# The opening of a two-layer conditioned decoder trunk: statistics first, all transposes ahead of the products, modulation pieces in pairs of quarters, a first chunk of six tiles

## The chip, the cores and the metric

The program runs on one core of one Trainium2 chip. The time is the device time of one execution in microseconds (us); lower is better. Engines are named as in the profile: PE is the matrix engine, DVE the vector engine, ACT the scalar engine, POOL the third elementwise engine, SP the engine whose queue issues most transfers (DMA).

## The reference

The reference is one inference step of a trunk of two layers, width 1024, over 256 prompt rows and 64 sample rows (8 samples of 8 rows), 320 rows in all. Each layer is a gated feed-forward block, four mixers side by side, and a second feed-forward block, each after a modulation whose scale, shift and gate come from a conditioning vector c, and each followed by a layer norm. The change touches only what happens before and in the first products of the first feed-forward block. Cut to that:

```python
def layer_norm(x, g, b, eps=1e-5):
    mu = jnp.mean(x, axis=-1, keepdims=True)
    var = jnp.mean(jnp.square(x - mu), axis=-1, keepdims=True)
    return (x - mu) * lax.rsqrt(var + eps) * g + b
def modulate(x, shift, scale):
    return x * (1.0 + scale[:, None, :]) + shift[:, None, :]
def swiglu(x, w_gate, w_up, w_down):
    return (jax.nn.silu(x @ w_gate) * (x @ w_up)) @ w_down
...
x = layer_norm(x, ln_in_g, ln_in_b)
for l in range(DEPTH):
    ada = (silu(c) @ w_ada[l] + b_ada[l]).reshape(b_, N_ADA, D_MODEL)
    sh1, sc1, g1, sh2, sc2, g2, sh3, sc3, g3 = [ada[:, i] for i in range(N_ADA)]
    h = swiglu(modulate(x, sh1, sc1), ffn1_w_gate[l], ffn1_w_up[l], ffn1_w_down[l])
    x = layer_norm(ALPHA * x + 0.5 * (1.0 + g1)[:, None, :] * h, post_ln_g[l, 0], post_ln_b[l, 0])
    ...
```

## The kernel before

All matrices are cut into tiles of 128 by 128. The 320 rows of x lie along the free axis and the 1024 features on the partitions, as eight tiles (k = 0 to 7) of 128x320. Each product is done in three matmuls, because weights and inputs are split into a high and a low part: high times high, low weight times high input, and high weight times low input. The tile names are `whi`, `wlo` for the weights and `xhi`, `xlo` for the inputs (`xhif`, `xlof` in the first feed-forward block).

The weights come from memory in the order in which the products use them. One load of 1 MB (`raw<-in_w_main`, called a pair here) holds two units of eight tiles each; a unit is split by one cast on ACT (`whi`, line 226) and one subtraction on DVE (`wlo`, line 234). The conditioning weights come as loads of 1 MB as well (`raw<-in_w_ada`, called pieces). SP issues all of them in one fixed order (`START = "aawaawaawaa"`, a for a piece, w for a pair), each when one of five buffers is free (`Stream.pump`).

The order of the instructions on every engine is the order in which the Python code calls them, and each engine works its queue off in that order. `next_unit`, which `tile` calls when a unit is used up, also splits units ahead by the table `AHEAD = (2, 2, 4, 4, 7, 8, 10)`: when unit 4 begins, units up to number 6 must be split, and those that aren't yet are split there.

The opening runs as follows. `setup` loads x with rows on the partitions (`xt`, three tiles), adds 1 to the bias table of the conditioning (`par`, two instructions on DVE, which wait for its load), then takes statistics of x and normalises it. `turn(k)` transposes feature tile k on PE (three matmuls into `xtp`), and `land(k)` copies it into SBUF. For the first feed-forward block the scale and the shift are made in quarters of 256 features: each quarter takes two pieces. One piece is 32 matmuls in the profile (`adp`, line 454, two calls of `ada_mm`), a copy by ACT (`adev`), and matmuls with a selection matrix (`adp<-sel,adev`, line 482, one selection for both pieces), whose result DVE adds to the bias table (line 491). From it `quarter(q)` makes A and B on DVE, then the modulated input tiles 2q and 2q+1: for the first of them ACT makes `xhi` directly, then come both `xff`, the second `xhi`, and DVE makes the two `xlo`.

`zchunk0` runs the first chunk: `kouter` goes over the eight k, and for each k over five weight tiles, each with its own PSUM bank (`zcf`, six banks in the ring `mm`). For one k it issues ten matmuls with `xhi`, then five with `xlo`. Between them lie the pieces of the next quarter, the selection and the last two transposes. After the odd k, `split_until(FIRST[q])` splits units up to 4, 6 and 7. After the chunk, `proj` makes the sixth tile (`uf`, m = 2) by itself, and the tiles from m = 3 on.

## Time and profile before

| | |
|---|---|
| three runs | 1305.42, 1308.83, 1309.57 us; median 1308.83 |
| span of the profiled execution, first to last instruction | 1308.1 us |
| PE busy | 1280.0 us, 98% of the span |
| DVE busy | 724.4 us, 55% |
| ACT busy | 556.6 us, 43% |
| mean granted clock of PE | 0.981 of full |

The page gives the span of the profiled execution, and no time of its own around it; the median of the runs lies 0.7 us above that span. A busy PE is a PE with a matmul in flight, whatever its clock.

### The profile page before, as it was taken

The page shows a single profiled execution, that of the slowest core. Times are in us where ns is not written, and L with a number is a line of the kernel's source. Part 1 is how long each engine was busy: PE and PEld are TensorE (multiplying, and loading weights), DVE is VectorE, ACT ScalarE, POOL GpSimd, SP SyncE. Part 2 cuts the span into 40 slices and gives each one's busy share as a digit, 9 for nine tenths or more (in the row PEclk, how much of TensorE's full clock was granted, in tenths as well). Part 3 has the DMA queues.
Part 4 walks back from the last instruction along what each step waited for, and adds up shares of the span by engine and source line. Part 5 has one row for each costly group of instructions (what it writes and reads, how often), then busy time and mean ns, then how long its engine had stood idle before and what let it go on. Part 6 is the DMA issues. An engine that isn't in the chain of part 4 may idle for free.

```text
span 1308.1 us, 22265 instructions
## 1 busy us (share of the span) xinstructions
PE 1280.0 (98%) x9382; PEld 1217.7 (93%) x9382; DVE 724.4 (55%) x1315; ACT 556.6 (43%) x878; POOL 33.4 (3%) x53
## 2 busy tenths in 40 slices
PE   6999999999999999999999999999999999999997
PEld 4999999989888999999999999999887999999997
DVE  4644444457976644444465444444697775444443
ACT  3643333337344633333445434333553455443432
POOL 0000000010010000000000000000100000000000
PEclk9999999999999999999999999999898989999998
DMA  9765656557879554554455454545387794444401
GB/s 353 275 233 206 211 193 237 207 159 247 325 259 121 188 202 178 199 185 163 166 185 196 164 183 172 190 174 180 113 287 286 115 197 157 140 158 152 143 29 41
DMA packets 51492, 247.46 MB, mean 189 GB/s; under 512 B 18656, under 2 KB 21168, under 8 KB 22208
## 3 DMA queue, kind: packets, MB, share of 16 engines
q1 hardware_dynamic: 46432, 244.33, 56.2%
q8 instruction: 73, 1.20, 0.4%
q0 software_dynamic: 512, 0.86, 0.4%
q10 hardware_dynamic: 4448, 0.84, 0.3%
q14 instruction: 27, 0.22, 0.1%
HBM read 243.45 MB, written 2.57 MB: 188 GB/s over the span
## 4 chain that ended last, share of the span: by engine, by line
PE 96%; DVE 1%; DMA 1%; ACT 1%; issue 0%; POOL 0%; SPq 0%; POOLq 0%; ACTq 0%; DVEq 0%
PE adp L459 4%; PE of L676 4%; PE oh L676 4%; PE oh L677 4%; PE of L677 4%; PE of L678 4%; PE oh L678 4%; PE uf L676 4%; PE uh L676 4%; PE uh L678 4%; PE uf L678 4%; PE uh L677 4%; PE uf L677 4%; PE gf L676 4%; PE gh L676 3%; PE gf L677 3%
## 5 line engine op out<-in xcount | busy, mean ns | idle before, releaser
L234 DVE TENSOR_TENSOR wlo<-raw,whi 128x1024 fp32r<-128x1024 f32 x312 | 372.8, 1222 | 135.9 <-ACT whi L226 134.6
L226 ACT CAST whi<-raw 128x1024 fp32r<-128x1024 f32 x312 | 315.6, 1045 | 28.7 <-issue 9.2
L676 PE MATMUL of<-hhf,whi 128*128 128x320 f32 x352 | 109.6, 311 | 0.0
L676 PE MATMUL oh<-hhh,whi 128*128 128x320 f32 x352 | 109.0, 310 | 0.0
L678 PE MATMUL of<-hhf,wlo 128*128 128x320 f32 x352 | 108.8, 309 | 0.0
L677 PE MATMUL of<-hlf,whi 128*128 128x320 f32 x352 | 108.8, 309 | 0.0
L678 PE MATMUL oh<-hhh,wlo 128*128 128x320 f32 x352 | 108.7, 309 | 0.0
L677 PE MATMUL oh<-hlh,whi 128*128 128x320 f32 x352 | 108.7, 309 | 0.0
L676 PE MATMUL uf<-xhif,whi 128*128 128x320 f32 x320 | 99.6, 311 | 0.0
L676 PE MATMUL uh<-xhih,whi 128*128 128x320 f32 x320 | 99.0, 309 | 0.0
L677 PE MATMUL uf<-xlof,whi 128*128 128x320 f32 x320 | 98.8, 309 | 0.0
L678 PE MATMUL uh<-xhih,wlo 128*128 128x320 f32 x320 | 98.8, 309 | 0.0
L677 PE MATMUL uh<-xloh,whi 128*128 128x320 f32 x320 | 98.8, 309 | 0.0
L678 PE MATMUL uf<-xhif,wlo 128*128 128x320 f32 x320 | 98.8, 309 | 0.0
L676 PE MATMUL gf<-xhif,whi 128*128 128x320 f32 x304 | 94.7, 312 | 0.0
L676 PE MATMUL gh<-xhih,whi 128*128 128x320 f32 x304 | 94.4, 310 | 0.0
L677 PE MATMUL gh<-xloh,whi 128*128 128x320 f32 x304 | 93.8, 309 | 0.0
L677 PE MATMUL gf<-xlof,whi 128*128 128x320 f32 x304 | 93.8, 309 | 0.0
L678 PE MATMUL gf<-xhif,wlo 128*128 128x320 f32 x304 | 93.8, 309 | 0.0
L678 PE MATMUL gh<-xhih,wlo 128*128 128x320 f32 x304 | 93.8, 309 | 0.0
L779 ACT CAST hhf<-sgf 128x320 fp32r<-128x320 f32 x44 | 20.2, 459 | 135.0 <-DVE sgf L776 135.0
L779 ACT CAST hhh<-sgh 128x320 fp32r<-128x320 f32 x44 | 20.2, 460 | 134.0 <-DVE sgh L776 134.0
(349 smaller groups left out, 2835.0 us busy)
## 6 DMA issues: line engine op xcount, KB each, us to landing
raw<-in_w_main SPq DMA_DIRECT2D x156, 1024.0 KB, 5.0
raw<-in_w_ada SPq DMA_DIRECT2D x72, 1024.0 KB, 4.9
out_yT<-x SPq DMA_DIRECT2D x8, 160.0 KB, 1.8
xt<-in_x SPq DMA_DIRECT2D x2, 512.0 KB
wsT<-in_wsT SPq DMA_DIRECT2D x2, 256.0 KB, 6.0
sgln<-in_sgln SPq DMA_DIRECT2D x2, 256.0 KB
cD<-in_pre_d POOLq DMA_DIRECT2D x4, 120.0 KB, 6.1
out_o_ds<-cD ACTq DMA_DIRECT2D x4, 120.0 KB
```

The source lines that it names most:

```text
L226: kk.nc.scalar.copy(hi, raw)
L234: self.kk.nc.vector.tensor_tensor(lo, raw, hi, op=ALU.subtract)
L459: nc.tensor.matmul(ps[32 * g:32 * g + 32, 0:w], self.cs[:, k, :], wt[:, h, g * w:(g + 1) * w], start=(k == 0), stop=(k == NK - 1))
L676: mm(ps, hi, xh, start=first, stop=False)
L677: mm(ps, hi, xl, start=False, stop=False)
L678: mm(ps, lo, xh, start=False, stop=last)
L779: nc.scalar.copy(hi, sg)
```

## The change

It changes the opening in five places.

- The two additions to the bias table come after the statistics and the normalisation of x in DVE's queue.
- All eight tiles of x are transposed ahead of the first product: two after the first piece, two after the second, four after the selection. Tiles 6 and 7 had their turn inside the first chunk before. `land` now says which engine copies.
- Ahead of the products stand two pieces where there were three.
- The two pieces of the next quarter are run one after the other, after the even k, and the selection and `quarter` lie inside the odd k, after the first three of its weight tiles; before, one piece lay ahead of the even k, one in it, and the selection ahead of the odd k.
- The first chunk has six tiles per k instead of five, so that each unit holds other tiles, and `uf` for m = 2 is made in it.

```diff
+CH0 = 6
...
-        for l in range(L):
-            a0 = PC[f"b_ada{l}"][0]
-            v = self.par[:, a0:a0 + 72].rearrange("p (i s k) -> p i s k", s=3, k=8)[:, :, 1:3, :]
-            nc.vector.tensor_scalar(v, v, 1.0, None, op0=ALU.add)
...
             nc.vector.tensor_scalar(xt[b][:n], xt[b][:n], mv[:n, b, 0:1], rs[:n, 3 + b:4 + b],
                                     op0=ALU.subtract, op1=ALU.mult)
+        for l in range(L):
+            a0 = PC[f"b_ada{l}"][0]
+            v = self.par[:, a0:a0 + 72].rearrange("p (i s k) -> p i s k", s=3, k=8)[:, :, 1:3, :]
+            nc.vector.tensor_scalar(v, v, 1.0, None, op0=ALU.add)
...
         st.ada(2)
         self.ada_adv(1)
+        turn(0)
+        land(0)
+        turn(1)
+        land(1)
         st.ada(2)
-        turn(0)
-        turn(1)
+        self.ada_adv(1)
+        turn(2)
+        turn(3)
+        land(2, True)
+        land(3)
         todo = st.split_hi(1)
         self.ada_adv(2)
-        land(0)
-        land(1)
         self.ada_adv(3)
-        for k in range(2, 6):
+        for k in range(4, 8):
             turn(k)
...
-    def kouter(self, x, banks, first, last, mid=None):
+    def kouter(self, x, banks, first, last, mid=None, at=None):
...
-        for w, b in zip(ws, banks):
+        for i, (w, b) in enumerate(zip(ws, banks)):
+            if mid and i == at:
+                mid()
             mm(b, w[0], xh, start=first, stop=False)
             mm(b, w[1], xh, start=False, stop=False)
-        if mid:
-            mid()
...
-        for k in range(2, 6):
-            land(k)
+        for k in range(4, 8):
+            land(k, k % 2 == 0)
         st.split_until(2)
-        banks = [self.mm(f"zc{nm}{i}") for i in range(CH)]
-        def piece():
-            st.ada(2)
-            self.ada_adv(1)
+        banks = [self.mm(f"zc{nm}{i}") for i in range(CH0)]
 
         for q in range(4):
-            if q < 3:
-                piece()
-            self.kouter(self.xk(2 * q), banks, q == 0, False, piece if q < 3 else None)
-            if q < 3:
+            def params():
                 self.ada_adv(3)
                 quarter(q + 1)
-            self.kouter(self.xk(2 * q + 1), banks, False, q == 3)
-            if q < 2:
-                turn(6 + q)
-                land(6 + q)
+
+            self.kouter(self.xk(2 * q), banks, q == 0, False)
+            if q < 3:
+                st.ada(4)
+                self.ada_adv(1)
+            self.kouter(self.xk(2 * q + 1), banks, False, q == 3, params if q < 3 else None, CH0 // 2)
             if q < 3:
                 st.split_until(FIRST[q])
...
-            if m == 2:
-                pg = b[4]
-            else:
-                pg = self.proj(self.mm(f"g{nm}{m}"))
-            glu(m, pg, self.proj(self.mm(f"u{nm}{m}")))
+            pg = b[2 * m] if 2 * m < len(b) else self.proj(self.mm(f"g{nm}{m}"))
+            pu = b[2 * m + 1] if 2 * m + 1 < len(b) else self.proj(self.mm(f"u{nm}{m}"))
+            glu(m, pg, pu)
...
-        tiles += _ffn_tiles(a["ffn1_w_gate"][l], a["ffn1_w_up"][l], a["ffn1_w_down"][l], CH)
+        tiles += _ffn_tiles(a["ffn1_w_gate"][l], a["ffn1_w_up"][l], a["ffn1_w_down"][l], CH if l else CH0)
```

**First place: PE, from its first instruction.** `adp` is a piece, `xtp` a transposed tile, `xt_72` to `xt_74` the three tiles of x. Before:

```order
L454 MATMUL adp_127<-raw_86,cs 32x128 x16
L454 MATMUL adp_148<-raw_88,cs 32x128 x16
L376 MATMUL xtp_167<-ident,xt_72 128x128
L376 MATMUL xtp_167<-ident,xt_73 128x128
L376 MATMUL xtp_167<-ident,xt_74 128x64
L376 MATMUL xtp_171<-ident,xt_72 128x128
L376 MATMUL xtp_171<-ident,xt_73 128x128
L376 MATMUL xtp_171<-ident,xt_74 128x64
L482 MATMUL adp_127<-sel,adev_146 128x18
L482 MATMUL adp_148<-sel,adev_179 128x18
```

Now:

```order
L459 MATMUL adp_127<-raw_86,cs 32x128 x16
L377 MATMUL xtp_148<-ident,xt_72 128x128
L377 MATMUL xtp_148<-ident,xt_73 128x128
L377 MATMUL xtp_148<-ident,xt_74 128x64
L377 MATMUL xtp_154<-ident,xt_72 128x128
L377 MATMUL xtp_154<-ident,xt_73 128x128
L377 MATMUL xtp_154<-ident,xt_74 128x64
L459 MATMUL adp_160<-raw_88,cs 32x128 x16
L377 MATMUL xtp_181<-ident,xt_72 128x128
L377 MATMUL xtp_181<-ident,xt_73 128x128
```

The two first transposes moved ahead of the second piece.

**Second place: PE, where the first chunk uses the second pair of weights for the first time** (`whi_353` before, `whi_366` now; `adp<-sel` is the selection from which the next tiles' parameters come). Before, this is in k = 3, after the selection of the third quarter:

```order
L690 MATMUL zcf_249<-xlof_328,whi_239 128x320
L482 MATMUL adp_363<-sel,adev_382 128x18
L482 MATMUL adp_394<-sel,adev_413 128x18
L685 MATMUL zcf_245<-xhif_318,whi_239 128x320
L686 MATMUL zcf_245<-xhif_318,wlo_240 128x320
L685 MATMUL zcf_246<-xhif_318,whi_353 128x320
L686 MATMUL zcf_246<-xhif_318,wlo_354 128x320
L685 MATMUL zcf_247<-xhif_318,whi_353 128x320
```

Now it is the fifth weight tile of k = 2, in the second quarter:

```order
L693 MATMUL zcf_258<-xhif_338,wlo_252 128x320
L692 MATMUL zcf_259<-xhif_338,whi_251 128x320
L693 MATMUL zcf_259<-xhif_338,wlo_252 128x320
L692 MATMUL zcf_260<-xhif_338,whi_251 128x320
L693 MATMUL zcf_260<-xhif_338,wlo_252 128x320
L692 MATMUL zcf_261<-xhif_338,whi_366 128x320
L693 MATMUL zcf_261<-xhif_338,wlo_367 128x320
```

The selection of the second quarter stands 20 products ahead of that row now. ACT's queue from that selection on reads the same as before, with other numbers: the two copies of pieces, `quarter`, and behind them the casts of the second pair:

```order
L483 COPY adev_319<-adp_281 128x128
L483 COPY adev_321<-adp_300 128x128
L651 ACTIVATE xhif_338<-x_189,B_220,A_219 128x256
L654 CAST xhif_338<-xff_337 128x64
L651 ACTIVATE xff_337<-x_189,B_220,A_219 128x256
L651 ACTIVATE xff_339<-x_191,B_220,A_219 128x256
L657 CAST xhif_340<-xff_339 128x320
L227 CAST whi_366<-raw_144 128x1024
L227 CAST whi_370<-raw_144 128x1024
```

The use of the second pair moved nearer to the selection, its casts did not.

**Third place: DVE, at the parameters of the fourth quarter** (line 491, now 496; `raw_267` before and `raw_298` now is the third pair of weights, `raw_411` the fourth). Before:

```order
L234 TENSOR_TENSOR wlo_467<-raw_267,whi_466 128x1024
L234 TENSOR_TENSOR wlo_471<-raw_267,whi_470 128x1024
L491 TENSOR_TENSOR ada_105<-adp_476,par 128x18
L491 TENSOR_TENSOR ada_105<-adp_507,par 128x18
L514 TENSOR_TENSOR A_207<-ada_105,par 128x18
L515 TENSOR_TENSOR s_537<-ada_105,par 128x18
```

Now:

```order
L235 TENSOR_TENSOR wlo_480<-raw_298,whi_479 128x1024
L235 TENSOR_TENSOR wlo_484<-raw_298,whi_483 128x1024
L235 TENSOR_TENSOR wlo_550<-raw_411,whi_549 128x1024
L496 TENSOR_TENSOR ada_103<-adp_507,par 128x18
L496 TENSOR_TENSOR ada_103<-adp_526,par 128x18
L519 TENSOR_TENSOR A_219<-ada_103,par 128x18
```

The low part of unit 6, first of the fourth pair, moved ahead of the two additions; on ACT its cast moved ahead of the fourth quarter in the same way. It is `next_unit` that puts it there: unit 4 now begins with the third weight tile of k = 5, just ahead of that selection.

## Rows read from the trace of the kernel before

**Rows 1.** Page, part 4: the chain that ended last, shares by engine.

```profile
PE 96%; DVE 1%; DMA 1%; ACT 1%; issue 0%; POOL 0%; SPq 0%; POOLq 0%; ACTq 0%; DVEq 0%
```

**Rows 2.** Timeline, PE, opening: start us, length, line, tiles, count, [idle before, releaser].

```profile
11.40 1.94 PE L454 MATMUL adp<-raw,cs 128*32 128x128 f32 x32 [11.40 <-DMA raw<-in_w_ada]
13.80 1.93 PE L454 MATMUL adp<-raw,cs 128*32 128x128 f32 x32 [0.46 <-DMA raw<-in_w_ada]
15.66 1.90 PE L376 MATMUL xtp<-ident,xt 128*128 128x128 f32 x6
...
18.36 3.70 PE L376 MATMUL xtp<-ident,xt 128*128 128x128 f32 x12
22.00 1.93 PE L454 MATMUL adp<-raw,cs 128*32 128x128 f32 x32
23.86 0.64 PE L685 MATMUL zcf<-xhif,whi 128*128 128x320 f32 x1
```

**Rows 3.** Timeline, PE, first chunk: the same columns.

```profile
24.56 0.47 PE L685 MATMUL zcf<-xhif,whi 128*128 128x320 f32 x1
...
26.43 0.47 PE L686 MATMUL zcf<-xhif,wlo 128*128 128x320 f32 x1
26.82 1.08 PE L454 MATMUL adp<-raw,cs 128*32 128x128 f32 x32
27.84 1.00 PE L690 MATMUL zcf<-xlof,whi 128*128 128x320 f32 x5
28.68 0.52 PE L482 MATMUL adp<-sel,adev 128*128 128x18 f32 x4
...
29.27 0.30 PE L686 MATMUL zcf<-xhif,wlo 128*128 128x320 f32 x1
...
30.44 0.31 PE L686 MATMUL zcf<-xhif,wlo 128*128 128x320 f32 x1
...
32.84 0.41 PE L685 MATMUL zcf<-xhif,whi 128*128 128x320 f32 x1
33.09 0.31 PE L686 MATMUL zcf<-xhif,wlo 128*128 128x320 f32 x1
...
51.07 0.37 PE L406 MATMUL bmean<-apar,o 128*128 128x112 f32 x2
51.21 0.39 PE L676 MATMUL uf<-xhif,whi 128*128 128x320 f32 x1
...
54.82 0.31 PE L676 MATMUL gf<-xhif,whi 128*128 128x320 f32 x1
```

**Rows 4.** Timeline, DVE, input statistics: the same columns.

```profile
8.07 0.28 DVE L346 TENSOR_SCALAR par<-par 128x48 f32<-128x48 f32 x2 [6.85 <-DMA par<-in_par]
...
11.12 1.23 DVE L357 BATCH_NORM_STATS2 bsx<-xt 64x6 f32<-64x512 f32 x2
...
13.78 2.25 DVE L363 TENSOR_SCALAR xt<-xt,mvx,rsx 128x1024 f32<-128x1024 f32 x3 [1.00 <-POOL rsx L360]
```

**Rows 5.** Timeline, ACT, second quarter of the modulation: the same columns.

```profile
27.97 0.27 ACT L478 COPY adev<-adp 128x128 f32<-128x128 f32 x1 [3.71 <-PE adp L454]
...
30.46 0.23 ACT L649 CAST xhif<-xff 128x64 fp32r<-128x64 f32 x1
...
32.08 2.00 ACT L226 CAST whi<-raw 128x1024 fp32r<-128x1024 f32 x2
```

**Rows 6.** Timeline, DVE, second quarter of the modulation: the same columns.

```profile
29.00 0.40 DVE L491 TENSOR_TENSOR ada<-adp,par 128x18 f32<-128x18 f32 x2 [4.27 <-PE adp L482]
...
33.16 2.36 DVE L234 TENSOR_TENSOR wlo<-raw,whi 128x1024 fp32r<-128x1024 f32 x2
```

**Rows 7.** Page, part 6: loads of the weights, KB each, us to landing.

```profile
raw<-in_w_main SPq DMA_DIRECT2D x156, 1024.0 KB, 5.0
```

**Rows 8.** Timeline, PE, after the first mixer: the columns of rows 2.

```profile
422.34 0.42 PE L685 MATMUL zch<-xhih,whi 128*128 128x320 f32 x1 [2.01 <-ACT xhih L649]
```

**Rows 9.** Windows: us, busy (count) by engine, PEclk, DMA share, GB/s.

```profile
419.00:422.50 3.50, 1.49 (x19) 0.71 (x19) 2.59 (x8) 0.97 (x3) 0.00 (x0) 0.95 0.88 335
422.50:426.00 3.50, 3.50 (x15) 3.50 (x16) 2.98 (x12) 3.33 (x7) 0.00 (x0) 0.54 0.99 405
```

More of the change, by code (lines that the diff above doesn't have):

```diff
@@ L367, in setup @@
         st.keep = 999
-        zs = []
+        zs = [None] * NK
         pts = {}
@@ L376, in turn, with land @@
                 nc.tensor.transpose(pt[:, b * P:b * P + n], xt[b][:n, k * P:(k + 1) * P], self.ident[:n, :n])
-        def land(k):
-            z = c.tile([P, N], F32, tag="res", bufs=8, name=f"x{k}")
-            if k % 2:
+        def land(k, act=False):
+            z = zs[k] = c.tile([P, N], F32, tag="res", bufs=8, name=f"x{k}")
+            if act:
                 nc.scalar.copy(z, pts.pop(k)[:, 0:N])
@@ L383, in land @@
                 nc.vector.tensor_copy(z, pts.pop(k)[:, 0:N])
-            zs.append(z)
         st.ada(2)
         self.ada_adv(1)
+        turn(0)
+        land(0)
+        turn(1)
+        land(1)
         st.ada(2)
-        turn(0)
-        turn(1)
+        self.ada_adv(1)
[3 more added lines that the diff above has]
+        land(3)
         todo = st.split_hi(1)
         self.ada_adv(2)
-        land(0)
-        land(1)
         self.ada_adv(3)
-        for k in range(2, 6):
+        for k in range(4, 8):
             turn(k)
-        return zs, todo, turn, land
+        return zs, todo, land
     def setup2(self):
@@ L719, in zchunk, with zchunk0 @@
         return banks
-    def zchunk0(self, nm, gb, todo, turn, land):
+    def zchunk0(self, nm, gb, todo, land):
         st = self.st
```

## The prediction

> **What bounds the kernel now.** I read three views in this order. First the chain of work that ended last: PE carries 96% of it [rows 1], so only time that PE waits, works at a low clock, or spends on switching counts. Then PE's timeline of the opening [rows 2]. PE starts at 11.40 us with the first piece, pauses 0.46 us for the load of the second, and from 13.80 on has no idle time in the opening: two transposes, selection, four transposes, third piece, first product at 23.86. What the change can save there is that pause and the order of the work behind it. Last the spacing of the products [rows 3], which tells the clock. From 24.56 to 26.43 seven products of 128x320 are 0.267 us apart, which is 320 columns at 1.2 GHz; from 29.27 to 30.44 eight are 0.147 apart, the level of 2.4 GHz. Pieces show the same: 1.86 us at 22.00, 1.02 at 26.82. So the clock rose at about 26.8, some 2.9 us after the first product.
>
> I compare one point before and after: the first product of `gf` for m = 3, at 54.82 before [rows 3]. Ahead of it lie the same 144 products either way (120 in the chunk and 24 of `uf` before, 144 in the chunk now), 8 pieces, 8 transposed tiles, 4 selections.
>
> **To the first product.** Taken out: the pause (0.46) and the third piece, 22.00 to 23.86 (1.86). Added: two transposed tiles, at 3.64 us for four (18.36 to 22.00), 1.82 [rows 2]. The first product comes at 23.86 - 0.46 - 1.86 + 1.82 = 23.36.
>
> This needs x normalised when the first piece ends, at 13.26. Before, the third tile's statistics began at 11.12, in an unbroken run behind the two additions of 8.07, and the three normalised tiles were done from 13.78 to 16.03 [rows 4]. The loads of x stand ahead of the pieces in SP's queue, and two pieces land 2.4 us apart (11.40, 13.80); by that estimate x is there at 9.0. The statistics then end 2.1 us earlier and the third tile is normalised at 13.9, when PE, at 0.30 us a transpose, asks for it (13.26 + 0.61). I take no wait. If nothing moved, PE would wait to 15.66, 2.4 us; those are the bounds. The two additions themselves (0.28 us) now stand ahead of DVE's first copies, while PE transposes; without that cover they cost 0.28.
>
> **The first quarter.** With the clock up at 26.8 as before, 12.9 products go by at 0.267, the other 5.1 of the 18 take 0.75: 27.55. Two pieces at 1.02 [rows 3] end at 29.59. Six products behind a piece take 0.25 for the first (32.84 to 33.09) and 0.147 for the others: 0.98. The selection, called s, starts at 30.57.
>
> From one selection to the next, without a wait: the start of the second product comes 0.59 after s (28.68 to 29.27), the twelfth ends at s + 2.21, 18 products of the even k take 2.65, two pieces 2.04, six products 0.98: 7.88. Two such steps, then 2.21, 36 products (5.29) and the bias means (51.07 to 51.21, 0.14) end at 30.57 + 15.76 + 2.21 + 5.29 + 0.14 = 53.97. Against 54.82 that is a **gain of 0.85 us**, from the pause and from fewer switches between pieces and products.
>
> **First wait: the second pair of weights.** The new order uses it in the fifth weight tile of k = 2, at s + 2.21 + 8 x 0.147 = s + 3.38, its low part at s + 3.53. ACT casts it behind the whole second quarter and DVE subtracts behind both `xlo`. Those queues are as before, so I read them from s = 28.68: the modulated tile is cast at 30.69 (s + 2.01) and ACT begins the pair at 32.08 [rows 5]; DVE begins its subtractions at 33.16 and ends the first of the two, half of 2.36 us, at 34.34 [rows 6], which is s + 5.66. PE, there at s + 3.53, waits **2.13 us**, in two parts around one product. Before, this pair was first used after the next two pieces, and the same work was hidden. The tile k = 2 itself is in time: s + 2.01 against s + 2.21. Units 4 and 5 are first wanted 7.6 us after the selection behind which they are cast (2.21 + 2.65 + 2.04 + 0.25 + 3 x 0.147), so there is no wait. Bounds: none if PE came 2.13 us later, 2.3 with a hand-over.
>
> **Second wait: unit 6 ahead of the fourth quarter.** ACT's copy of the last piece starts 0.13 us after the piece's end and takes 0.27 (27.84, 27.97), so it ends at s - 0.58; the cast of unit 6 (half of 2.00 us) ends at s + 0.42, DVE's subtraction starts 0.08 later (33.16 against 33.08) and takes 1.18: s + 1.68. The additions for the quarter, due at s + 0.32 (29.00 against 28.68), are queued behind it and come 1.36 late, and A, B and `xhi` of k = 6 with them: s + 3.37 instead of s + 2.01 [rows 5, 6]. PE is there at s + 2.21 and waits **1.16 us**. This supposes that the fourth pair has landed. SP issues it when the pieces of the third quarter are read, some 38.6; with 5.0 us to landing [rows 7], and 2.4 for one load ahead of it, that is 46.0, and ACT asks at s - 0.58 = 47.9 (s = 48.46). Bounds: none if unit 6 were split behind the quarter, and every microsecond that the load is later adds one.
>
> The copies of x, the later loads of pieces and the third gate behind the chunk I take at nothing: units 6 and 7 are split by the chunk's end and give 48 products, 7.1 us, in which ACT and DVE work off three gates and reach unit 8. Without that cover it would be one split, 2.2 us.
>
> **Sum.** -0.85 + 2.13 + 1.16 = +2.44. The profiled span of 1308.1 becomes 1310.5; the median of the runs lies 0.7 above that span, so I forecast **1311.2** against 1308.83.
>
> **Rivals.**
> - *The clock.* At 422.34 a product came after a pause of 2.01 us, PE had been busy 1.49 of 3.50 us, and over the next 3.50 the granted clock was 0.54 [rows 8, 9]. The first wait is as long, though with a product in the middle. If it drops the clock, or if the clock after the first product rises one such stretch later (one record of 2.9 us says little), it costs 3.50 x 0.46 = 1.6: 1312.8; with both 1314.4. The Trainium skill (TensorE: Matmul & The Clock Gate, "Why this matters for your kernels") warns only of longer pauses; by it the wait costs no clock and the sum stands. The row speaks against it, but for another mix of work.
> - *The waits are hidden.* PE arrives late enough at both places; the gain alone is left, 1308.0. It needs PE 2.13 us later after the selection, or ACT and DVE as much earlier, and no row shows either.
> - *The other side: faster.* PE now works unbroken from 11.40. If that raises the clock at time r instead of 26.8, it gains half of 26.8 - r; below 1304.9 (0.3%) it decides from r = 14.2. Against it: from 13.80 to 23.86 PE was never idle and stayed at the low level [rows 2, 3]. The Trainium skill (the same page, "Part 1: The HAM clock gate") has it that activity releases the throttle; taken alone that rule would speak for this rival, the row speaks against it.
> - *x comes late.* PE waits up to 2.4 us at the first transpose: 1313.6 at most. The loads' order speaks against it.
>
> **How the numbers follow.** Both waits as worked out: 0.50, its own range 1310.0 to 1312.8. Clock: 0.25. Hidden: 0.12. Early clock: 0.05. Late x: 0.08. The range reaches from the gain alone, less half a microsecond (1307.5), to both parts of the clock (1314.4). 0.3%, 3.9 us, is about what a measurement of this kernel can tell from no change: faster is below 1304.9, slower above 1312.7. Faster: 0.03 of the early clock and 0.02 of the hidden waits, 0.05. Slower: 0.19 of the clock, 0.06 of the first case, 0.05 of late x, 0.30. The rest, 0.65, is within.
>
> **What would show it.** The first product should start near 23.4, with no PE idle time from 11.40 on. In k = 2 PE's idle time should name the cast (1.1 us) and then the subtraction of the second pair (1.0); at k = 6 it should name `xhi`, 1.2, with DVE's subtraction of unit 6 ahead of the additions. `gf` for m = 3 should start at 57.3, and everything behind it should keep its length. I am wrong if `gf` starts before 55, if PE waits for a load in the chunk, or if the chain's shares move later in the program.

## The result and the profile after

The changed kernel takes 1316.39 us in the median of four runs (1313.86 to 1316.71), against 1308.61 for the kernel before. The ratio on record is 1.0070, interval 1.0042 to 1.0099; it is not the quotient of these two medians, which is 1.0059, and the same holds for the ratios below. Measured twice more it came out at 1.0068 (1.0037 to 1.0099) and 1.0044 (1.0010 to 1.0079). It is slower by half a per cent or somewhat more, 6.7 to 11.0 us by the three pairs of medians; the forecast was 2.4 us slower. Two slow runs, one of the changed kernel (1323.87 us) and one of `e3` below (1321.57 us), are left out of all means.

| | before | changed |
|---|---|---|
| span of the profiled execution | 1308.1 us | 1315.0 us |
| PE busy | 1280.0 us | 1284.5 us |
| mean granted clock of PE | 0.981 | 0.978 |
| `gf` for m = 3 starts | 54.82 us | 59.36 us |
| from there to the end of the span | 1253.28 us | 1255.64 us |

Of the 6.9 us between the spans 4.54 lie ahead of `gf`, where the change is, and 2.36 behind it, where it changes nothing. The page's chain, shares by engine, of the changed kernel (to be held against [rows 1]):

```profile
PE 95%; DVE 2%; ACT 1%; DMA 1%; issue 0%; POOL 0%; another core or an unknown queue 0%; POOLq 0%; SPq 0%; ACTq 0%; DVEq 0%
```

By these rounded shares PE lost a point to DVE, which PE had not waited for in the opening. PE's timeline of the opening says where (columns as in [rows 2]):

```profile
11.93 1.93 PE L459 MATMUL adp<-raw,cs 128*32 128x128 f32 x32 [11.93 <-DMA raw<-in_w_ada]
13.80 0.86 PE L377 MATMUL xtp<-ident,xt 128*128 128x128 f32 x2
14.89 1.28 PE L377 MATMUL xtp<-ident,xt 64*128 64x64 f32 x4 [0.24 <-DVE xt L360]
16.10 1.93 PE L459 MATMUL adp<-raw,cs 128*32 128x128 f32 x32
...
24.30 0.63 PE L692 MATMUL zcf<-xhif,whi 128*128 128x320 f32 x1
...
26.87 0.38 PE L693 MATMUL zcf<-xhif,wlo 128*128 128x320 f32 x1
27.08 0.31 PE L692 MATMUL zcf<-xhif,whi 128*128 128x320 f32 x1
...
28.34 1.95 PE L459 MATMUL adp<-raw,cs 128*32 128x128 f32 x64
...
31.21 0.52 PE L487 MATMUL adp<-sel,adev 128*128 128x18 f32 x4
...
34.44 0.31 PE L693 MATMUL zcf<-xhif,wlo 128*128 128x320 f32 x1
35.72 0.42 PE L692 MATMUL zcf<-xhif,whi 128*128 128x320 f32 x1 [0.97 <-ACT whi L227]
36.98 0.44 PE L693 MATMUL zcf<-xhif,wlo 128*128 128x320 f32 x1 [0.84 <-DVE wlo L235]
37.23 0.45 PE L692 MATMUL zcf<-xhif,whi 128*128 128x320 f32 x1
...
39.48 2.50 PE L459 MATMUL adp<-raw,cs 128*32 128x128 f32 x64
...
42.89 0.52 PE L487 MATMUL adp<-sel,adev 128*128 128x18 f32 x4
...
47.84 1.95 PE L459 MATMUL adp<-raw,cs 128*32 128x128 f32 x64
...
50.71 0.52 PE L487 MATMUL adp<-sel,adev 128*128 128x18 f32 x4
...
53.83 0.42 PE L692 MATMUL zcf<-xhif,whi 128*128 128x320 f32 x1 [0.75 <-ACT xhif L654]
...
59.36 0.39 PE L681 MATMUL gf<-xhif,whi 128*128 128x320 f32 x1
```

Three things are new here: a short wait for the normalised x at 14.89, the two waits that were forecast (35.72 with 36.98, and 53.83), and a clock that falls behind the first of them. The fall is read from lengths: the 64 matmuls of two pieces take 2.50 us at 39.48, and 1.95 at 28.34 and 47.84. A table by stretch shows the granted clock (columns as in [rows 9]):

```profile
34.80:37.20 2.40, 0.64 (x2) 0.41 (x3) 1.94 (x3) 1.81 (x2) 0.00 (x0) 1.00 0.57 236
37.20:40.60 3.40, 3.40 (x33) 2.99 (x36) 0.86 (x1) 0.00 (x0) 0.00 (x0) 0.51 0.39 111
40.60:44.00 3.40, 3.40 (x63) 3.20 (x56) 0.66 (x5) 0.53 (x2) 0.00 (x0) 0.99 0.96 337
```

In the wait PE worked 0.64 of 2.40 us. Over the next 3.40 it worked without a pause, but at 0.51, the level of 1.2 GHz, and did about half of what it does at full clock. So the first wait costs its own length and then up to 1.7 us more.

What held PE there are ACT's casts and DVE's subtractions of the second pair and of unit 6, as forecast. First ACT, then DVE:

```profile
34.62 1.99 ACT L227 CAST whi<-raw 128x1024 fp32r<-128x1024 f32 x2
...
50.02 1.05 ACT L227 CAST whi<-raw 128x1024 fp32r<-128x1024 f32 x1
```

```profile
9.87 1.28 DVE L354 BATCH_NORM_STATS2 bsx<-xt 64x6 f32<-64x512 f32 x2 [0.62 <-DMA xt<-in_x]
...
12.59 2.25 DVE L360 TENSOR_SCALAR xt<-xt,mvx,rsx 128x1024 f32<-128x1024 f32 x3 [1.00 <-POOL rsx L357]
14.76 0.27 DVE L365 TENSOR_SCALAR par<-par 128x48 f32<-128x48 f32 x2
...
35.70 2.36 DVE L235 TENSOR_TENSOR wlo<-raw,whi 128x1024 fp32r<-128x1024 f32 x2 [0.46 <-ACT whi L227]
...
51.10 1.23 DVE L235 TENSOR_TENSOR wlo<-raw,whi 128x1024 fp32r<-128x1024 f32 x1 [1.36 <-ACT whi L227]
52.25 0.25 DVE L496 TENSOR_TENSOR ada<-adp,par 128x18 f32<-128x18 f32 x2
```

The first two rows of DVE answer to [rows 4]: with the additions behind them the statistics no longer wait for those, but the third tile's statistics waited 0.62 for the load of x itself.

Behind `gf` low clock shows too. Two stretches of the changed kernel, and below them the same places in the program in the kernel before (4.5 us earlier):

```profile
289.80:293.20 3.40, 3.40 (x21) 2.47 (x20) 1.61 (x5) 0.00 (x0) 2.83 (x7) 0.50 0.12 21
675.50:678.90 3.40, 3.40 (x24) 2.01 (x24) 1.67 (x6) 0.00 (x0) 0.85 (x1) 0.50 0.01 2
```

```profile
285.20:288.60 3.40, 3.23 (x44) 2.18 (x48) 2.57 (x9) 0.51 (x1) 2.85 (x7) 1.00 0.34 53
671.00:674.40 3.40, 2.89 (x40) 1.60 (x32) 2.56 (x8) 1.10 (x3) 0.80 (x1) 1.00 0.51 137
```

The same code runs there at 0.50 in one execution and at 1.00 in the other, and each such stretch can cost up to 1.7 us, so the 2.36 us can be low clock. Whether that belongs to the change is one question for the experiments.

### The profile page after: what moved, and what is told of

The parts are those of the page before. It is cut to its first block, busy times and chain, and to the rows that moved or that the text cites. A ratio compares the mean times of both kernels' runs of the same rounds, so it can differ in the third digit from the quotient of the medians.

```text
span 1315.0 us, 22265 instructions
## 1 busy us (share of the span) xinstructions
PE 1284.5 (98%) x9382; PEld 1220.3 (93%) x9382; DVE 726.2 (55%) x1316; ACT 556.1 (42%) x877; POOL 34.2 (3%) x53
## 4 chain that ended last, share of the span: by engine, by line
PE 95%; DVE 2%; ACT 1%; DMA 1%; issue 0%; POOL 0%; another core or an unknown queue 0%; POOLq 0%; SPq 0%; ACTq 0%; DVEq 0%
PE adp L464 5%; PE of L681 4%; PE oh L681 4%; PE oh L683 4%; PE of L682 4%; PE of L683 4%; PE oh L682 4%; PE uh L681 4%; PE uf L681 4%; PE uh L682 4%; PE uh L683 4%; PE gf L681 3%; PE uf L683 3%; PE uf L682 3%; PE gh L681 3%; PE gf L683 3%
```

## The experiments

The theory: the two waits cost what was forecast, and the first one drops the clock as well. The rivals: the new order of the opening itself costs the time; or the whole program, by lying 4.5 us later, meets the clock differently. No kernel leaves computation out. Those with `fill` or `warm` in their diff run additional products whose result nothing uses.

All runs together, in groups of one kernel, taken on several chips. Within a group a run is 0.97 us shorter for each 0.001 of mean granted clock (fitted over all 308 runs; correlation -0.91). The last column moves every run along that line to a clock of 0.980, so that it shows what isn't in the granted clock. The record of the clock begins with its first rise: the stretch ahead of it counts as 1.00 (in the changed kernel up to 27.0 us, with products 0.267 us apart), so a late first rise stays in the last column. Intervals there are 95%; those of the column before it are 1.8 to 3.3 us either way.

| kernel | runs | mean clock | ratio to before | mean, less before's | at equal clock |
|---|---|---|---|---|---|
| before | 146 | 0.9807 | 1.0007 (again) | 0 (1307.5) | 0 |
| changed | 27 | 0.9781 | 1.0070, 1.0068, 1.0044 | +7.3 | +4.8 ± 0.9 |
| `e1` second pair early | 10 | 0.9788 | 1.0023 | +3.7 | +1.9 ± 1.7 |
| `e2` unit 6 behind | 10 | 0.9812 | 1.0016 | +3.3 | +3.9 ± 1.3 |
| `e3` both | 11 | 0.9815 | 0.9997 | +0.1 | +0.9 ± 1.0 |
| `e4` first wait filled | 10 | 0.9826 | 1.0007 | +2.4 | +4.2 ± 1.3 |
| `c1` five tiles | 12 | 0.9822 | 0.9998 | -0.2 | +1.2 ± 0.8 |
| `d1` before, 4.6 us later | 12 | 0.9817 | 1.0043 | +3.7 | +4.6 ± 1.9 |
| `f1` changed, 1.8 us later | 12 | 0.9803 | 1.0050 | +8.2 | +7.8 ± 1.1 |
| `e5` both, and x in two parts | 22 | 0.9812 | 0.9981, 0.9985 | -1.8 | -1.3 ± 0.8 |
| `w1` before, PE busy early | 12 | 0.9809 | 0.9982 | -1.5 | -1.2 ± 0.9 |
| `w2` `e3`, PE busy early | 12 | 0.9798 | 0.9974 | -1.3 | -2.1 ± 1.1 |
| `g1` `e5`, PE busy early | 12 | 0.9782 | 1.0002 | -0.8 | -3.2 ± 0.8 |

In the last three the record begins at 6 to 7 us, so low clock of the opening counts in their mean clock, and their last column can't be held against the others. The means of the kernel before on the four chips lie between 1306.6 and 1308.7 us; on the two chips where both ran side by side the changed kernel is 9.3 and 5.8 us behind, and `f1` on its chip 7.0. The expectations of `e1`, `e2` and `e4` counted from the 1316.4 us of the changed kernel's first four runs, and the medians came out 2.6, 4.8 and 4.4 us below the expected times. The mean of all 27 runs is 1314.8, so the first four stood high, and how much each edit is worth is read from the traces.

### The second pair of weights ahead of the chunk

```diff
-        st.split_until(2)
+        st.split_until(4)
```

> The changed kernel with units 2 and 3 split ahead of the first product instead of behind the second quarter; unit 6 stays ahead of the fourth quarter. Theory (wait, and the clock that falls after it): PE's first wait in k = 2 (0.97 + 0.84 us in the changed kernel) is gone, and with it the stretch of low clock behind it, which made the step from the second selection to the third 11.7 us instead of 7.8; from selection to selection 7.9 us, gf of m = 3 near 55.6 instead of 59.4, time near 1312.8. Rival (the wait costs only itself, the low clock comes from the pieces and the order of the work): the step shrinks by 1.8 us only, gf near 57.6, time near 1314.6.

1310.19 us, 1.0023 (0.9993 to 1.0053); `gf` at 54.14. The first wait is gone, no low stretch follows k = 2, selections lie 7.8 us apart, and the wait at k = 6 stays (0.75 for `xhif`). `gf` came 1.5 us earlier than expected; the clock had risen at 19.3 in this profile (more below).

### Unit 6 behind the fourth quarter

```diff
-AHEAD = (2, 2, 4, 4, 7, 8, 10)
+AHEAD = (2, 2, 4, 4, 6, 8, 10)
```

> The changed kernel with unit 6 split behind the fourth quarter (the table's entry for unit 4 is 6 instead of 7). Theory: only PE's wait at k = 6 goes (0.75 us), the first wait and the low clock stay; gf of m = 3 near 58.5, time near 1315.6. Rival (the queue order there costs nothing on PE, the parameters were late for another reason): no change of either.

1310.77 us, 1.0016 (0.9986 to 1.0046); `gf` at 58.76 against 58.5. The wait at k = 6 is gone. The first wait stays (0.95 and 0.84), and behind it the clock is at 0.50 from 38.0 to 41.4. Taking out one wait saves 3.5 (`e1`) and 3.9 us (`e2`) of 7.3 by the means, but each with an interval of 3 us either way, so these don't say how the loss divides. The traces do: from the fourth selection to `gf` it takes 7.63 us here (51.13 to 58.76) and 8.65 in the changed kernel, so the second wait is worth 1.02 us; the first one with its fall is worth 3.87 (11.68 us from selection to selection in the changed kernel, 7.81 in `e1`).

### Both edits

> Both edits. Theory: the opening keeps only the gain that was worked out, gf of m = 3 between 54.0 and 55.0 (54.8 before the change, depending on when the loads land), and since the rest of the program is the same work at the same place in time, the time is that of the kernel before within 1.5 us, 1307 to 1310. Rival (the new order costs something lasting behind the opening, 2 to 3 us from gf on): gf in the same place but the time stays at 1310.5 or more.

1308.70 us, 0.9997 (0.9963 to 1.0032); `gf` at 53.04. Neither wait is left in the chunk; there is only one of 0.19 at its second product, for the low part of the first pair, as in `e1` and `e4`. The means fall from +7.3 to +0.1, at equal clock from +4.8 to +0.9 ± 1.0: most of the loss comes from the two waits and what they bring. That the new order of the opening itself costs the time is refuted but for 1.9 us at most, by that interval.

### The first wait filled with products

Unused products take the place of the idle time, six ahead of the high product and five ahead of the low one. The wait's length stays, only PE doesn't stand still.

```diff
...
+            fill = self.fill and i == 4
+            if fill:
+                d = self.rn("fill")
+                for _ in range(6):
+                    mm(d[:, 0:N], xh[:, 0:P], xh, start=True, stop=True)
             mm(b, w[0], xh, start=first, stop=False)
+            if fill:
+                for _ in range(5):
+                    mm(d[:, 0:N], xh[:, 0:P], xh, start=True, stop=True)
```

> The changed kernel with 11 products of 128x320 into a spare bank, whose result is not used, put into the first wait: 6 ahead of the product that waits for the cast and 5 ahead of the one that waits for the subtraction. The wait of the useful work stays as long. Theory (the idle time drops the clock): no stretch of low clock after it, the step from the second selection to the third is 10.0 instead of 11.7 us, time 1.7 us below the changed kernel's, near 1314.7. Rival (the low clock has another cause): a low stretch all the same, the step stays at 11.7 and the time at 1316.4 or above.

1310.33 us, 1.0007 (0.9976 to 1.0037). PE's timeline of that place:

```profile
29.80 0.52 PE L488 MATMUL adp<-sel,adev 128*128 128x18 f32 x4
...
33.17 1.04 PE L697 MATMUL fill<-xhif 128*128 128x320 f32 x6
34.30 0.41 PE L698 MATMUL zcf<-xhif,whi 128*128 128x320 f32 x1
34.55 0.89 PE L701 MATMUL fill<-xhif 128*128 128x320 f32 x5
35.56 0.42 PE L702 MATMUL zcf<-xhif,wlo 128*128 128x320 f32 x1
...
37.09 1.95 PE L460 MATMUL adp<-raw,cs 128*32 128x128 f32 x64
...
39.95 0.52 PE L488 MATMUL adp<-sel,adev 128*128 128x18 f32 x4
```

The low product starts 5.76 us after its selection (29.80), as in the changed kernel (36.98 - 31.21 = 5.77). Behind it the pieces take 1.95 and not 2.50, and from selection to selection it is 10.15 us in place of 11.68. With the same useful work in the same order, but without PE standing still, no fall follows in this profile. One profile is thin evidence; the repeats below add to it. The kernel is at +2.4 us by the means, with 2.0 either way, and that this is the forecast's number is chance in part. At equal clock it stands where the changed kernel stands (+4.2, +4.8): what the filling saved is in the clock (0.9826 against 0.9781). One fall less is worth about 0.0013 of that (half of 3.4 us in 1315); the rest is not explained.

### The changed kernel and the kernel before, again

> The changed kernel once more, unaltered. The first four runs gave a median 7.8 us above the kernel before; the profiles account for 4.5 us up to gf of m = 3 and 2.4 us behind it, where nothing was changed. Theory (the part behind it is the clock, which falls at other places in each execution): over more runs the difference shrinks towards the opening's, 3 to 5 us (1311.5 to 1313.5 against 1308.3), and the later part lies between 1250 and 1256 us in the profile. Rival (the later part is a lasting cost of the change): the median stays 7 to 8 us above.

> The kernel before once more, unaltered, for the spread of two profiles of one program. Theory (the windows of the clock lie differently in each execution): the time agrees with the other runs of the kernel before within 1.5 us in the median, single runs spread over 10 us or more, and the profile shows the clock's rise or its low stretches at other places than the first one (26.8; 415.9, 422.8). Rival (the places are fixed by the program): the same places within 1 us.

> The changed kernel a third time, unaltered. In 16 runs its mean granted clock was 0.978, against 0.981 of 105 runs of the kernel before, and that is worth 3 us of the 8 us between the means; the other 5.7 us are there at the same granted clock. Theory (the 3 us are mostly chance, but for the fall behind the first wait): a granted clock of 0.979 or more and a mean difference of 5 to 7 us. Rival (they belong to the change): 0.978 or less again and 8 us or more.

1317.41 us, 1.0068 (1.0037 to 1.0099), the kernel before 1307.09, 1.0007 (0.9983 to 1.0030), and the changed kernel a third time 1313.75, 1.0044 (1.0010 to 1.0079). The profile of the first repeat is the exception to the fall. Its waits are the same, yet the pieces behind them are quick:

```profile
32.03 0.52 PE L487 MATMUL adp<-sel,adev 128*128 128x18 f32 x4
...
36.53 0.42 PE L692 MATMUL zcf<-xhif,whi 128*128 128x320 f32 x1 [0.95 <-ACT whi L227]
37.79 0.41 PE L693 MATMUL zcf<-xhif,wlo 128*128 128x320 f32 x1 [0.84 <-DVE wlo L235]
39.31 1.95 PE L459 MATMUL adp<-raw,cs 128*32 128x128 f32 x64
...
42.19 0.52 PE L487 MATMUL adp<-sel,adev 128*128 128x18 f32 x4
```

From selection to selection it took 10.16 us, against 11.68 in the first profile, so the fall itself costs 1.52 us. In the third profile the pieces take 2.52 us again. Of the five profiles with this wait left empty (three of the changed kernel, `e2`, `f1`) four show the fall. Of the eight profiles of the new opening in which PE doesn't stand still there (`e1`, `e3`, `e4`, `c1`, two of `e5`, `w2`, `g1`) none shows it. That ties the fall to the idle time; why it stays out in one of five is open. The part behind `gf` took 1255.64, 1255.7 and 1249.3 us in the three profiles of the changed kernel, 1253.28 and 1247.6 in the two of the kernel before, each with the same products on PE. It follows the low stretches of the execution, and the 2.36 us of the first pair are within that scatter. The medians of the repeats are 11.0 and 6.7 us behind: the first is not the 3 to 5 us that had been expected if the part behind `gf` were chance. The mean clock of the third set is 0.9785, a little less than the 0.979 that had been expected.

### The kernel before, 4.6 us later

31 unused products stand behind its first chunk. They shift everything after it without a wait.

```diff
+            d = self.rn("fill")
+            for _ in range(31):
+                nc.tensor.matmul(d[:, 0:N], self.xhi[0][:, 0:P], self.xhi[0], start=True, stop=True)
```

> The kernel before with 31 products of 128x320 into a spare bank, whose result is not used, between the first chunk and the sixth tile: 31 x 0.147 = 4.6 us, and nothing else changed. Theory (a shift of the program costs only itself in the median, single executions differ by the clock): 1308.3 + 4.6 = 1312.9 within 2 us. Rival (a shift moves the layer norms against the clock in a fixed way and so costs more, as the changed kernel lost 2.4 us behind the opening): 1315 or more.

1311.14 us, 1.0043 (1.0013 to 1.0073). `gf` moved to 59.00, the changed kernel's place, and at equal clock the kernel is 4.6 ± 1.9 us behind. A pure delay costs its length, and the place in the program alone doesn't bring more than 1.9 us beyond it.

### The changed kernel, 1.8 us later

Twelve such products at the same place of the changed kernel.

> The changed kernel with 12 products of 128x320 into a spare bank, not used, behind the first chunk: 1.8 us of pure shift. Theory (the changed kernel's lower granted clock, 0.978 against 0.981, is in the opening's fall and else chance): time 1.8 us above the changed kernel at the same granted clock, 1317.7 in the mean, and a granted clock between 0.977 and 0.981. Rival (its later stages stand badly against the clock, and a shift frees them): a granted clock of 0.981 or more and a time no higher than the changed kernel's, 1315 or less.

1315.30 us, 1.0050 (1.0026 to 1.0075); at equal clock 3.0 ± 1.3 us behind the changed kernel, for 1.8 of added work. The first wait comes ahead of the products, and the clock falls behind it as before (0.95 and 0.85 of idle time, then pieces of 2.38 us). The shift gave nothing back.

### The first chunk of five tiles

```diff
-CH0 = 6
+CH0 = 5
```

> The changed kernel with a first chunk of five tiles; everything else of the change stays. The second pair of weights is then first used in k = 3, as before the change, and unit 4 begins with k = 6. Theory (six tiles bring both waits, by where the units begin): no idle time of PE in the chunk, gf of m = 3 between 53 and 55, time between 1307 and 1310. Rival (the two pieces in one run and the selection inside the odd k bring the waits): the waits of about 1.8 and 0.8 us stay, time 1311 or more.

1308.31 us, 0.9998 (0.9975 to 1.0021); `gf` at 55.00, with no wait in the chunk. With five tiles per k the second pair is wanted after the next pieces, and unit 4 begins behind the fourth quarter's selection. So it is the sixth tile that brings both waits; transposing early and pairing the pieces does not. (The edit also puts the selection behind two weight tiles in place of three.) At equal clock `c1` is 1.2 ± 0.8 us behind the kernel before and `e3` 0.9 ± 1.0, so about 1 us may belong to the rest of the new order.

### x transposed in two parts

On top of both edits the third row tile of x, the one that is normalised last, is transposed only behind the second piece.

```diff
...
-        turn(0)
-        land(0)
-        turn(1)
-        land(1)
+        turn(0, (0, 1))
+        turn(1, (0, 1))
         st.ada(2)
         self.ada_adv(1)
+        turn(0, (2,))
+        land(0)
+        turn(1, (2,))
+        land(1)
```

> The changed kernel with both waits mended, and the third row tile of x transposed only behind the second piece, so that PE need not wait for it (0.24 us idle, and 2.30 us from the first piece to the second where two transposed tiles take 1.83). Theory (x lands late and costs 0.5 us of the gain): no idle time of PE between the first and the second piece, second piece 3.0 to 3.4 us after the first instead of 4.1, the first product 0.4 to 0.5 us earlier against the first piece. Rival (the second piece's load bounds it): PE waits for that load instead, and the first product comes no earlier.

> The mended changed kernel with the third row tile of x transposed behind the second piece, once more. At the same granted clock its ten runs lay 0.6 us below the kernel before, and two profiles whose clock rose at the same place (17.6) give 39.0 us from the first piece to gf of m = 3, against 39.4. Theory (the change without its two waits and without the wait for x is worth half a microsecond, which times cannot resolve): a ratio whose interval holds 1, and a time at the same granted clock 0 to 1.5 us below. Rival (it keeps losing to the kernel before, as the mended kernel with the wait for x did by 1.1 us): above the kernel before at the same granted clock.

1306.73 us, 0.9981 (0.9956 to 1.0007), and 1305.63, 0.9985 (0.9959 to 1.0012). PE's timeline of the second set:

```profile
11.37 1.93 PE L463 MATMUL adp<-raw,cs 128*32 128x128 f32 x32 [11.37 <-DMA raw<-in_w_ada]
13.23 1.12 PE L379 MATMUL xtp<-ident,xt 128*128 128x128 f32 x4
14.28 1.38 PE L463 MATMUL adp<-raw,cs 128*32 128x128 f32 x32
...
27.22 0.62 PE L491 MATMUL adp<-sel,adev 128*128 128x18 f32 x4 [0.84 <-ACT adev L487]
```

PE no longer waits for x, and starts the second piece 2.91 us after the first, with no idle time, where the changed kernel took 4.17. In the first set's profile and in that of the kernel before (again) the clock rose at the same time, 17.65 and 17.6, so the two can be held against each other: from the first piece to the first product 9.28 us (12.07 to 21.35) against 9.74 (11.86 to 21.60). That is 0.46 less; the forecast had 0.50, but for a third piece of 1.86 us, which took 1.01 behind this early rise, so that the agreement is luck in part. At `gf` 0.37 is left (39.03 us from the first piece, against 39.40). By the means this is the best version of the study, 1.8 us ahead, and neither interval leaves 1 out.

The second set also shows what the edit of `e1` can cost. The casts of the second pair stand ahead of the copies of the pieces in ACT's queue now, and the quicker opening reaches them before their load has landed:

```profile
25.01 1.99 ACT L227 CAST whi<-raw 128x1024 fp32r<-128x1024 f32 x2 [2.80 <-DMA raw<-in_w_main]
26.91 0.43 ACT L487 COPY adev<-adp 128x128 f32<-128x128 f32 x2
```

So the selection at 27.22 waited 0.84 us, the next tile another 0.26, and `gf` started at 51.10 in both sets, though the first piece of the second set started 0.70 earlier.

### PE busy ahead of the first load

44 unused products on a constant tile fill PE's time before the first piece, in the kernel before (`w1`), in `e3` (`w2`) and in `e5` (`g1`).

```diff
...
+        for _ in range(44):
+            nc.tensor.matmul(wp[:, 0:N], warm[:, 0:P], warm[:, 0:N], start=True, stop=True)
```

> The kernel before with 44 products of 128x320 on a constant tile ahead of the first piece, in the time in which PE waits for the loads; their result is not used. Theory (the opening runs at the low clock because PE has done no products yet): the clock rises ahead of the first piece, pieces take 1.0 us from the start, the first product comes near 20 instead of 23.9 (then bound by the loads), gf of m = 3 near 50 instead of 54.8 or 51.3, time 3 to 5 us below the kernel before. Rival (transposes and pieces let the clock fall again before the first product, or the loads bound the opening anyway): gf between 53 and 55, no difference in the time.

> The changed kernel with both waits mended (units 2 and 3 split ahead, unit 6 behind the fourth quarter) and the same 44 products ahead of the first piece. Theory: as for the kernel before with them; gf near 49.5, time 4 to 6 us below the kernel before, since the eight transposes in a row then run at the high clock. Rival (eight transposes with no product between them let the clock fall, as in three profiles where it had risen at 19 and fell at 22.7): the first pieces are fast, a low stretch lies around the first product, gf at 51 or later and the time no better than with the kernel before warmed.

> The same kernel with the 44 products on a constant tile ahead of the first piece. In two kernels these products raised the clock at 6 to 7.4, but it fell again at 14.2 and 16.3, when PE had waited for the loads and then run pieces and transposes. Theory (nothing that is done ahead of the loads keeps the clock up): at the same granted clock within 1.5 us of the kernel without them, a low stretch around the second piece. Rival (with the order that waits least the clock stays up): no low stretch ahead of gf, gf at 49.5 or earlier, 1304 or less.

1308.70 us, 0.9982 (0.9952 to 1.0012); 1306.89, 0.9974 (0.9941 to 1.0007); 1306.68, 1.0002 (0.9973 to 1.0031). The clock rises early, at 7.4, 6.0 and 6.1 us, but it doesn't last. PE of `w1`, and the stretch behind:

```profile
11.72 1.08 PE L460 MATMUL adp<-raw,cs 128*32 128x128 f32 x32 [0.66 <-DMA raw<-in_w_ada]
14.20 1.94 PE L460 MATMUL adp<-raw,cs 128*32 128x128 f32 x32 [1.40 <-DMA raw<-in_w_ada]
```

```profile
14.20:17.60 3.40, 3.40 (x37) 2.24 (x37) 2.51 (x4) 1.02 (x2) 0.00 (x0) 0.50 1.02 424
```

The quicker first piece only waits longer for the second load, 1.40 us, and the clock is low again. In `w2` it fell at 16.3 for 10.2 us, in `g1` at 19.7 for 3.4; there PE waits for the normalised x between the pieces (0.43, 0.40 and 0.39 us in `w2`, 0.19 and 0.39 in `g1`). `gf` came at 51.22, 53.56 and 51.24, not at the 50 and 49.5 of the theories of `w1` and `w2`. The loads and x set the pace ahead of the first product, and the clock was low again before it in `w2` (it started at 23.04) and just behind it in `g1` (19.15). In `w1` the clock was up again from 17.6 us, as in the kernel before (again), and `gf` came at the same place (51.22, 51.26). `g1` is 1.9 us below `e5` at equal clock, more than the 1.5 expected, but that column doesn't hold for it; by the means it is 1.0 us above.

## Why the prediction was wrong

The forecast of 1311.2 was 5.2 us below the median. Its direction and both waits were right; the step that failed is that the sum put the clock behind the first wait at nothing. The fall stood among the rivals with a chance of 0.25, and happens in four profiles of five. It costs 1.5 us and doesn't make up the 5.2: even the rival with both parts of the clock, 1314.4, lies 2.0 below the median. The sentence that everything behind `gf` should keep its length failed too, by 2.36 us in the first pair, which lies within the scatter that the repeats show. Luck has little part in the miss: over all runs both kernels are lower, by 1.3 and 1.6 us (1307.5 and 1314.8), and the difference is 7.3 us where 2.4 was forecast.

**To the first product: forecast 23.36, seen 24.30.** The first load landed 0.53 later, which is no part of the change (it lands between 11.31 and 12.14 with either opening). Two transposed tiles took 2.30 us (13.80 to 16.10) where 1.82 were forecast. "I take no wait" failed: the estimate had x landing at 9.0, the trace has the third tile's statistics beginning at 9.87 after a wait for that load, and the tiles normalised until 14.84 and not 13.9. This is the rival of a late x at a fifth of its bound, 0.48 of 2.4 us. `e5` shows that it can be had back.

**The first quarter.** The clock rose at 27.0, by products 0.267 apart up to 26.87 and 0.15 apart from 27.08 on. The selection came 6.91 us after the first product; the forecast had 7.21.

**First wait: right.** The casts began at s + 3.41 (forecast s + 3.40), the subtractions at s + 4.49 (s + 4.48), with s = 31.21. PE's product at 35.72 came 1.28 after the one before it and that at 36.98 another 1.26, where 0.147 is the spacing without a wait: 2.25 us late in all, forecast 2.13.

**Behind the first wait: the failed step.** From selection to selection the sum had 7.88 + 2.13 = 10.01 us, the trace 11.68. Of the 1.67 between them 1.52 is the low stretch (the repeat without the fall took 10.16), the rest the somewhat longer wait. The rival had priced it at 1.6, from the one row that spoke for it [rows 8, 9], and it was put second because that pause had no product in its middle. `e4` and the count of profiles with and without the wait tie it to the idle time, and two steps of 0.97 and 0.84 us with 0.42 of work between them were enough in four profiles of five. The Trainium skill (TensorE: Matmul & The Clock Gate, "Why this matters for your kernels") warns only of longer pauses in that section; the measurement differs, with the clock at 0.51 behind these, and decides.

**Second wait: right, somewhat smaller.** 1.02 us against 1.16, by the way to `gf` with and without it (8.65 in the changed kernel, 7.63 in `e2`); 0.75 of it is idle time. The additions came at s + 1.54 (forecast s + 1.68), with s = 50.71, the modulated tile was complete at s + 3.07 (s + 3.37), and PE was there at s + 2.37 (s + 2.21). The fourth pair had landed in time.

**What stands behind the chunk, at nothing: right.** From the fourth selection to `gf` it took 8.65 us with the second wait in it, forecast 8.80, and no other wait is seen. The gain of 0.85 is partly there at best: `e3`, without the two waits, is level with the kernel before, and in the one pair of profiles with the same first rise `e5`, which also takes the wait for x out, has 0.37 at `gf`. Its means (-1.8 ± 1.8 us, at equal clock -1.3 ± 0.8) are too wide to tell 0.37 from 0.85.

**The sum by these pieces.** `gf` moved by 4.54 us: the forecast's 2.44, 1.67 behind the first wait, 0.53 of the later load, 0.48 of x, less 0.3 in the first quarter and 0.3 in other steps. What the single profile can't decide is the rest. By the means of all runs the changed kernel is 7.3 us behind: 4.8 at equal clock, 2.5 by a lower mean clock (0.9781 against 0.9807). One low stretch as at 37.2 is worth 0.0013 of the mean clock, so the fall behind the first wait, in four profiles of five, explains 0.8 x 0.0013 of that or 1.0 us. Open are the other 1.5, and the 1.8 us by which 4.8 exceeds what the opening shows without the fall (4.54 - 1.52 = 3.02). A later first rise of the clock would be part of that, since it stays in the equal-clock column: it came at 26.8, 17.6 and 25.3 in three profiles with the old opening, and at 27.0, 29.2 and 26.1 in those of the changed kernel. Of the six other profiles that open like the changed kernel, `e2`, `f1` and `c1` had it at 27.7, 26.5 and 27.4, but `e1`, `e3` and `e4` at 19.1 to 19.3: six late of nine, against two of three. That doesn't tell the openings apart, and it stays open. In `e3`, without the waits, both are gone to within their intervals.

**The rivals.** The waits were not hidden. The early clock didn't come in any profile of the changed kernel. The statement that 0.3% is what a measurement can tell was fair for medians of a dozen runs, but single runs of the kernel before lay between 1297 and 1320 us, so that the three runs given at first had shown much less scatter than there is.

## What to carry to other kernels

When work is regrouped, ask for each tile of weights when it is first used and where its preparation stands in the queues of the other engines: one tile more per step moved two first uses ahead of their casts. A wait on the matrix engine is to be priced at its length plus the low clock that may follow it, here 2.25 us and in most executions another 1.5, and a wait broken by one product is still a wait. Work that is moved ahead in a queue to mend one wait can hold up what stands behind it, as the casts in the second set of `e5` did. Gains of a microsecond in the opening can't be seen in totals whose single runs spread over 20 us; read them from one fixed product in the trace, between profiles whose clock rose at the same place, and correct the totals for the granted clock.

## What the runs showed of the hardware

- The first rise of the clock isn't fixed by the kernel. With the same opening it came at 17.6 us in one profile and at 26.8 in another, and that moved `gf` from 51.26 to 54.82.
- A rise can be lost at once. In `e1` the clock rose at 19.3 while PE did transposes, four selections and twelve more transposes, the first product came at 22.23, and the clock was low from 22.7 to 26.1. The table by stretch of that kernel:

```profile
19.30:22.70 3.40, 3.34 (x19) 2.11 (x18) 2.96 (x12) 2.64 (x6) 0.00 (x0) 1.00 1.01 422
22.70:26.10 3.40, 3.28 (x12) 3.28 (x13) 3.10 (x7) 3.40 (x6) 0.00 (x0) 0.50 0.77 313
```

PE was busy for 3.34 of 3.40 us ahead of the fall, and the clock fell all the same. `e3` and `e4` show the same fall at 22.6 and 22.7. Yet in the kernel before (again) and the first set of `e5` the clock rose at 17.6, PE did the same twelve transposes behind it, and no fall came in the opening. What decides it stays open.
- The time of this program goes with its mean granted clock: 0.97 us for 0.001, over spans from 1292.8 (0.993) to 1315.0 us (0.978) in the profiles.
- The load that the first piece waits for landed at 11.3 to 12.1 us in the profiles without warm-up products, with either opening. A place in the opening is therefore best counted from the start of the first piece.
